# A row gradient in three slots: the second and third load of each group become one transfer

## The chip, the cores and the metric

The kernel runs on one core of one Trainium2 chip. The metric is the device time of one execution in microseconds (us). A core has engines that run instruction streams of their own; here VectorE (DVE) does the arithmetic, GpSimd (POOL) some very small operations, and SyncE (SP) issues all transfers between the chip's main memory (HBM) and its working memory (SBUF, 128 partitions). TensorE and ScalarE do nothing. A transfer is issued by one instruction on SP and is carried by 16 DMA engines; its semaphore says when all of it has landed.

## The reference

```python
x = np.random.randn(8192, 8192).astype(np.float32)
return np.gradient(x, axis=1)
```

Each row is differentiated along its 8192 columns: inside, `(x[j+1] - x[j-1]) / 2`; at the two ends, the plain differences `x[1] - x[0]` and `x[8191] - x[8190]`. The input and the output have 268.44 MB each.

## The kernel before

The 8192 rows are cut into 32 tiles (`nsets`) of 256 rows: 128 partitions with R = 2 rows each, so a tile has W = 16384 numbers, 64 KB, in each partition, 8.39 MB in all. Tiles come in groups of NB = 3. Within a group, partition p holds six rows that follow each other in HBM; tile k of the group is the k-th pair of them. `x_sets[i]` and `out_sets[i]` are the views of tile i in the input and the output. The last group has two tiles.

Three slots of SBUF (`slot0` to `slot2`) hold a tile each; tile i lies in slot i % 3, from element SH = 64 on. The result of a tile is written into the same slot, 64 elements further down, from element 0 on, and is stored from there. [...]

What happens with tile i, with the lines that do it:

- `load(i)` (line 55) issues its load on SP. From tile 3 on it needs the store of tile i - 3 to have landed, as that frees the slot.
- Line 65: POOL takes the four plain differences at the ends of the two rows into `ends`. It waits for the load.
- Line 71: DVE makes half the difference of the two neighbours, over the whole 16382 numbers at once. It waits for POOL's four differences, and so for the load.
- Line 82: the four end values are copied over the result's ends, on POOL for some tiles (i % 5 is 1 or 3, but not the last two tiles), on DVE for the others.
- Line 84: SP issues the store of the slot.

The order is written by hand (`tc.manual_schedule()`): each engine runs its instructions in the order of the program. SP's queue so reads: loads of tiles 0, 1, 2; stores 0, 1, 2; loads 3, 4, 5; stores 3, 4, 5, and so on. An instruction that waits holds back all that stand behind it in its engine's queue. `chain` names for each step the earlier step that it needs; the order of all else within a slot follows from that.

Of the kernel before, what the change touches and what calls it, by code (L numbers as in the profile page):

```python
# [1 line left out]

# [4 lines left out]


@with_exitstack
def kernel(  # L10
    ctx: ExitStack,
    tc: tile.TileContext,
    x: bass.AP,
    out: bass.AP,
):
    nc = tc.nc
    P = nc.NUM_PARTITIONS
    n, m = x.shape
    R = 2
    NB = 3  # L20
    SH = 64
    W = R * m
    nsets = n // (P * R)
    f32 = x.dtype

    def sets(a):
        found = []
        for first in range(0, nsets, NB):
            q = min(NB, nsets - first)
            rows = a[first * P * R : (first + q) * P * R, :].rearrange("(p q) m -> p (q m)", p=P)  # L30
            found += [rows[:, k * W : (k + 1) * W] for k in range(q)]
        return found

    x_sets, out_sets = sets(x), sets(out)

    pool = ctx.enter_context(tc.tile_pool(name="pool", bufs=1))
    pad = pool.tile([P, 32], f32, name="pad", tag="pad")
    slots = [pool.tile([P, SH + W], f32, name=f"slot{k}", tag=f"slot{k}") for k in range(NB)]
    ends = pool.tile([P, nsets, R, 2], f32, name="ends", tag="ends")
    loads, stores = [], [None] * nsets  # L40
    in_front = {}

    def chain(i, ins, *needed):
        group, engine = f"slot{i % NB}", ins.ins.engine
        keep = [o.ins for o in needed]
        if in_front.get(engine, (None,))[0] == group:
            keep.append(in_front[engine][1])
        tc.declare_no_dep(ins.ins, group=group, keep=keep, reason="implied by the needed step")
        tc.add_to_no_dep_group(group, ins.ins)
        in_front[engine] = group, ins.ins  # L50
        return ins

    def load(i):
        b = slots[i % NB]
        ins = nc.sync.dma_start(out=b[:, SH : SH + W], in_=x_sets[i])  # L55
        loads.append(chain(i, ins, *([stores[i - NB]] if i >= NB else [])))

    with tc.manual_schedule():
        for i in range(NB):
            load(i)  # L60
        for i in range(nsets):
            b = slots[i % NB]
            xin = b[:, SH : SH + W].rearrange("p (t m) -> p t m", m=m)

            ins = nc.gpsimd.tensor_sub(  # L65
                out=ends[:, i, :, :],
                in0=xin[:, :, 1 : m : m - 2],
                in1=xin[:, :, 0 : m - 1 : m - 2],
            )
            at = [chain(i, ins, loads[i])]  # L70
            ins = nc.vector._custom_dve(  # L71
                dve_ops.TENSOR_TENSOR_REDUCE_SUB_MAX,
                out=b[:, 1 : W - 1],
                in0=b[:, SH + 2 : SH + W],
                in1=b[:, SH : SH + W - 2],
                s0=0.0,
                s1=0.5,
            )
            halved = chain(i, ins, *at)
            res = b[:, 0:W].rearrange("p (t m) -> p t m", m=m)  # L80
            placer = nc.gpsimd if i % 5 in (1, 3) and i < nsets - 2 else nc.vector
            ins = placer.tensor_copy(out=res[:, :, 0 : m : m - 1], in_=ends[:, i, :, :])  # L82
            placed = chain(i, ins, halved)
            ins = nc.sync.dma_start(out=out_sets[i], in_=b[:, 0:W])
            stores[i] = chain(i, ins, placed)
            if i % NB == NB - 1:
                for k in range(i + 1, min(i + 1 + NB, nsets)):
                    load(k)


# [1 line left out]
_INS = ['x']  # L92
_OUTS = [((8192, 8192), 'float32')]


# [23 lines left out]
```

## Time and profile before

| | |
|---|---|
| time, median of 3 runs | 1246.33 us (1245.98 to 1246.47) |
| the profiled execution: time | 1246.23 us |
| the profiled execution: span, first to last instruction | 1244.3 us |
| DVE busy | 554.6 us, 45% of the span |
| POOL busy | 8.9 us, 1% |
| one pass of line 71 on DVE | 17.22 us, 32 times |
| transfers issued on SP | 32 loads and 32 stores |
| load, issue to landing, median | 57.9 us |
| store, issue to landing, median | 40.4 us |
| moved over the span | 431 GB/s in the mean |

Each line of the profile's groups names a line of the kernel, an engine and an operation with what it writes and reads. "Waits" give who waited for whom, with the total, the number of times and the longest. The timeline gives start and duration in us; what was idle before, and what ended that idle time, stands in square brackets; several issues that follow each other are merged into one line with their number. "SPq" is SP's instruction queue, "to landing" the time from an issue to the moment when all of its data is there. The trace also holds a record of each DMA packet with its start, duration and size, from which the movement of a single DMA engine can be followed.

### The profile page before, as it was taken

Reading aid. Unit: us, or ns where it says so; the run is one execution under the profiler, and the core shown is the slowest. Engines: PE = TensorE matmul, PEld = TensorE weight load, DVE = VectorE, ACT = ScalarE, POOL = GpSimd, SP = SyncE. Lnnn points to the kernel's source line nnn. Section 1 sums busy time; section 2 is a strip of 40 time slices with the busy share of each in tenths; the row PEclk is TensorE's granted clock in tenths of the full one; section 3 lists DMA queues with packets and bytes.
Section 4 is the critical chain, followed back from the end, with each engine's and each line's share of the span. In section 5 each row is a group of like instructions: output and inputs, shape, how many; then the busy total and the mean of one; then the engine's idle time right before and its main releaser. Section 6 shows DMA issues by size and latency. Waiting matters only on the chain.

```text
span 1244.3 us, 237 instructions
## 1 busy us (share of the span) xinstructions
DVE 554.6 (45%) x52; POOL 8.9 (1%) x48
## 2 busy tenths in 40 slices
DVE  2850583069009603850582079009603840591082
POOL 0000000000000000000000000000000000000000
DMA  9999999999999999999999999999999999999999
GB/s 404 438 436 423 421 438 438 438 438 436 434 423 430 434 438 438 430 436 432 428 434 436 432 436 434 438 436 430 432 428 438 436 434 438 434 434 430 430 409 404
DMA packets 9217, 536.88 MB, mean 431 GB/s; under 512 B 1024, under 2 KB 1024, under 8 KB 1024
## 3 DMA queue, kind: packets, MB, share of 16 engines
q1 hardware_dynamic: 9216, 536.88, 99.8%
q14 instruction: 1, 0.01, 0.0%
HBM read 268.44 MB, written 268.44 MB: 431 GB/s over the span
## 4 chain that ended last, share of the span: by engine, by line
another core or an unknown queue 74%; DVE 18%; DMA 3%; issue 2%; POOL 1%; SPq 0%; POOLq 0%
DVE slot L71 18%; DMA slot<-in_x_dram 3%; POOL ends L65 0%; POOL slot L82 0%; SPq L55 0%; POOLq L114 0%; DVE slot L82 0%
## 5 line engine op out<-in xcount | busy, mean ns | idle before, releaser
L71 DVE CUSTOM_DVE_ANT_0 slot<-slot 128x16382 f32<-128x16382 f32 x32 | 551.2, 17224 | 667.2 <-POOL ends L65 667.2
L65 POOL TENSOR_TENSOR ends<-slot 128x4 f32<-128x4 f32 x32 | 6.4, 200 | 988.1 <-DMA slot<-in_x_dram 988.1
L82 POOL COPY slot<-ends 128x4 f32<-128x4 f32 x12 | 2.3, 192 | 207.9 <-DVE slot L71 207.9
L82 DVE COPY slot<-ends 128x4 f32<-128x4 f32 x20 | 3.4, 172 | 0.7
L103 POOL MEMSET const-bfloat16-1.0<- 128x1 bf16 x1 | 0.1, 102 | 0.0
L103 POOL MEMSET const-uint8-127<- 128x1 uint8 x1 | 0.1, 102 | 0.0
L103 POOL MEMSET const-float32-0.0<- 128x1 f32 x1 | 0.1, 99 | 0.2 <-issue 0.2
L103 POOL MEMSET const-float32-1.0<- 128x1 f32 x1 | 0.1, 99 | 0.0
## 6 DMA issues: line engine op xcount, KB each, us to landing
slot<-in_x_dram SPq DMA_DIRECT2D x32, 57.9
out_dram<-slot SPq DMA_DIRECT2D x32, 40.4
```

The lines of the kernel that those rows point to most:

```text
L65: ins = nc.gpsimd.tensor_sub(out=ends[:, i, :, :], in0=xin[:, :, 1 : m : m - 2], in1=xin[:, :, 0 : m - 1 : m - 2],)
L71: ins = nc.vector._custom_dve(dve_ops.TENSOR_TENSOR_REDUCE_SUB_MAX, out=b[:, 1 : W - 1], in0=b[:, SH + 2 : SH + W], in1=b[:, SH : SH + W - 2],
L82: ins = placer.tensor_copy(out=res[:, :, 0 : m : m - 1], in_=ends[:, i, :, :])
L103: nc = _bacc.Bacc("TRN2", target_bir_lowering=False, num_devices=1)
```

## The change

The first slot becomes a tile of its own (`one`), and the second and third become one SBUF tile (`two`) that holds both, each with its 64 elements of room ahead as before. The first tile of a group is loaded as before. The second and third are loaded by one transfer of 2 x 64 KB a partition (`load_rest`): in HBM the two pieces follow each other directly, in SBUF they lie a slot apart. This transfer needs the stores of both tiles that were in the two slots before it. The last group, which has two tiles, loads them one by one as before. The stores, the arithmetic and the order of compute stay.

```diff
-    slots = [pool.tile([P, SH + W], f32, name=f"slot{k}", tag=f"slot{k}") for k in range(NB)]
+    one = pool.tile([P, SH + W], f32, name="one", tag="one")
+    two = pool.tile([P, NB - 1, SH + W], f32, name="two", tag="two")
+    slots = [one] + [two[:, k, :] for k in range(NB - 1)]
...
     def load(i):
-        b = slots[i % NB]
-        ins = nc.sync.dma_start(out=b[:, SH : SH + W], in_=x_sets[i])
+        ins = nc.sync.dma_start(out=slots[i % NB][:, SH : SH + W], in_=x_sets[i])
         loads.append(chain(i, ins, *([stores[i - NB]] if i >= NB else [])))
 
+    def load_rest(i):
+        rows = x[(i - 1) * P * R : (i + NB - 1) * P * R, :].rearrange("(p q) m -> p (q m)", p=P)
+        rest = rows[:, W : NB * W].rearrange("p (k w) -> p k w", w=W)
+        ins = nc.sync.dma_start(out=two[:, :, SH : SH + W], in_=rest)
+        for k in range(i, i + NB - 1):
+            chain(k, ins, *([stores[k - NB]] if k >= NB else []))
+            loads.append(ins)
+
+    def load_group(i):
+        load(i)
+        if i + NB <= nsets:
+            load_rest(i + 1)
+        else:
+            for k in range(i + 1, nsets):
+                load(k)
+
     with tc.manual_schedule():
-        for i in range(NB):
-            load(i)
+        load_group(0)
...
             if i % NB == NB - 1:
-                for k in range(i + 1, min(i + 1 + NB, nsets)):
-                    load(k)
+                load_group(i + 1)
```

## The prediction

> **What bounds the kernel now.** I read the page first (busy shares, slices, DMA queues), then the waits of the engines and of SP's queue, then the timeline of one group and of the last two tiles, and last the trace's DMA packet records, packet by packet.
>
> From the page:
>
> ```profile
> span 1244.3 us, 237 instructions
> DVE 554.6 (45%) x52; POOL 8.9 (1%) x48
> DMA  9999999999999999999999999999999999999999
> DMA packets 9217, 536.88 MB, mean 431 GB/s; under 512 B 1024, under 2 KB 1024, under 8 KB 1024
> q1 hardware_dynamic: 9216, 536.88, 99.8%
> ```
>
> DVE works less than half of the time; the one DMA queue has packets on its 16 engines for 99.8% of the span. The packet records give the grain: 8,192 packets of 65,536 B, eight per DMA engine and transfer, the median lasting 2.418 us and one starting 2.415 us after the other. So a transfer of one tile takes 8 x 2.415 = 19.32 us, load or store alike, and the 64 of them take 1,236.5 us of the 1,244.3. Only the rest, 7.8 us, can be won; anything that leaves the DMA engines without work costs directly.
>
> The waits, of the engines and then of SP's queue:
>
> ```profile
> POOL ends L65 <- DMA slot<-in_x_dram: 988.1, 32, 77.2
> DVE slot L71 <- POOL ends L65: 667.2, 32, 60.1
> ...
> SPq L84 <- DVE slot L82: 525.5, 20, 55.9
> SPq L55 <- DMA out_dram<-slot: 372.9, 29, 19.1
> SPq L84 <- POOL slot L82: 299.0, 12, 36.7
> ```
>
> Columns: total us, times, longest. POOL waits for loads and DVE for POOL; SP waits for compute before stores and for stores before loads. These waits cost nothing as long as another transfer is in flight. Whether one is can be read from one group in the timeline (tiles 3, 4, 5, which I call A, B, C: slots 0, 1, 2):
>
> ```profile
> 139.69 0.20 POOL L65 TENSOR_TENSOR ends<-slot 128x4 f32<-128x4 f32 x1 [77.15 <-DMA slot<-in_x_dram]
> 139.92 17.22 DVE L71 CUSTOM_DVE_ANT_0 slot<-slot 128x16382 f32<-128x16382 f32 x1 [59.92 <-POOL ends L65]
> 157.21 0.19 POOL L82 COPY slot<-ends 128x4 f32<-128x4 f32 x1 [17.32 <-DVE slot L71]
> 157.43 39.24 SPq L84 DMA_DIRECT2D out_dram<-slot  x3
> 159.01 0.20 POOL L65 TENSOR_TENSOR ends<-slot 128x4 f32<-128x4 f32 x1 [1.60 <-DMA slot<-in_x_dram]
> ...
> 178.64 0.20 POOL L65 TENSOR_TENSOR ends<-slot 128x4 f32<-128x4 f32 x1 [19.44 <-DMA slot<-in_x_dram]
> ...
> 197.94 39.04 SPq L55 DMA_DIRECT2D slot<-in_x_dram  x3
> ```
>
> A, B and C land at 139.62, 158.94 and 178.58, a transfer apart. A's store is issued at 157.43 and lands at 197.92: it stood behind loads B and C, so the queue serves in order. At each issue one transfer is in flight and another queued. The one place where that fails is the end:
>
> ```profile
> 1185.59 0.20 POOL L65 TENSOR_TENSOR ends<-slot 128x4 f32<-128x4 f32 x1 [77.06 <-DMA slot<-in_x_dram]
> 1185.82 17.23 DVE L71 CUSTOM_DVE_ANT_0 slot<-slot 128x16382 f32<-128x16382 f32 x1 [59.83 <-POOL ends L65]
> 1203.08 0.17 DVE L82 COPY slot<-ends 128x4 f32<-128x4 f32 x1
> 1203.28 19.61 SPq L84 DMA_DIRECT2D out_dram<-slot  x2
> ```
>
> Tile 30 lands at 1185.52 while only load 31 is queued, and its store is issued 17.76 us later. In the packet records the last load packets end between 1201.39 and 1204.51 on the 16 engines, and the store's packets start between 1204.13 and 1204.52: the early engines stand idle up to 2.9 us, and the latest, which sets the end, has no gap.
>
> **The change, part by part.** The sum is made against the profiled execution: 1246.23 us, its span 1244.3 and 1.9 around it; it is 0.1 us under the median, 1246.33.
>
> *Fewer issues.* Twenty loads become ten. SP spends 0.34 us on each, 3.4 us in all, while it waits 1,197 us in the rows above: nothing. Between transfers the packet records show no gap (load 0 ends at 21.75 on the first engine, load 1 starts at 21.75): joining two loads removes no idle time.
>
> [...]
>
> *The joined transfer.* Per engine it has 16 pieces of 64 KB in place of two times 8: the two slots stay apart in SBUF, so no piece grows. No row shows this form, two pieces in one partition running. Above, it can't beat the packet pace (0 us gained); below, I take 0 too, since loads and stores, with opposite ends, already have the same 2.415. B's data is usable only when the slowest engine has finished both, one transfer (19.32) later than now.
>
> *Its double wait.* SP issues it when both store B and store C have landed, not B's at store B's landing. Behind the wait in SP's queue stands store A of the next group, due some 37 us later (load A 19.3, then 17.8). Load A, issued as soon as store C is, is in flight meanwhile: store C lands about 0.3 us after its last packet, an issue takes 0.85 to 1.0 us to its first packet (1203.28 to 1204.13), and load A lasts 19.3: 18 us to spare. Load A itself no longer waits at all, as store A lands before store C is issued.
>
> *Store B, the tight place.* When the pair lands, only store A is queued. Call M the moment when the slowest engine ends the pair. Store A keeps it busy until M + 19.32. Store B's first packet comes at M + 0.33 (last packet to landing: 1185.19 to 1185.52) + 17.76 (landing to issue, as for tile 30; 17.81 where POOL places the ends, as at 139.62 to 157.43) + 0.85 to 1.0 = M + 18.94 to 19.14. The slowest engine has 0.18 to 0.38 us to spare, in all ten groups. Faster engines run dry and wait; that costs nothing, as at the end of before. Cost 0, by a thin margin.
>
> [...]
>
> *C's compute.* It starts when DVE is through with B, not 2 us after it. Where POOL places B's ends (tiles 1, 13, 16, 28) C's subtraction stands behind that copy on POOL, some 0.5 us more. Store C is due at M + 38.6 and issued near M + 36. Nothing.
>
> *Drift, the only moving term.* The 16 engines don't run in step. At each change from load C to store A the last load packet is lengthened on some of them: by 1.02 us on the mean at the first change, then by 0.19, 0.02, 0.12, 0.30, 0.12, 0.13, 0.03, 0.00, 0.04; nowhere else by over 0.05 but at the start. The latest end moves from 62.00 (load 2) to 1204.51 (load 31), 59 transfers of 19.32 = 1139.88 later: 2.63 us of lengthening in nine changes, 0.29 each. In the new kernel the dry wait at store B brings the engines together again in each group, to within some 0.4 us. Then each change may cost what it costs engines in step: at least 0, at most 1.00 (the first change, latest end 41.68 to 62.00 less 19.32). I take 0.34, the second change (158.60 to 178.26 less 19.32): its engines lay 0.63 us apart and it is no first. 9 x (0.34 - 0.29) = +0.45 us.
>
> The last two tiles and the start are as before. Sum: 1246.23 + 0.45 = 1246.7 us.
>
> **The rivals.**
>
> *In step (slower).* Each change costs 1.00 like the first: 9 x (1.00 - 0.29) = +6.4, 1252.6 us. For it: then the engines lay 0.6 us apart, and the lengthening shrinks as the drift grows. Against it: at the second change they lay as close and it was a fifth; the first is also the first write of the program. It passes 0.2% from 0.57 us per change on. Chance 0.14.
>
> *Store B too late (slower).* If the path from the pair's last packet to store B's first is x longer than summed, ten groups lose 10 (x - 0.28). It passes 0.2% from x = 0.53 on; at 0.7 it gives 1250.4, and with no cover at all 10 x 17.8 = 178 us, 1424. For it: the margin is a hundredth of a group. Against it: every link was measured in this trace. [...]
>
> *The lengthening goes (faster).* In before, SP issues store B (176.7) just while the last packets of load C run (174.9 to 177.9); engines that ended before that issue were lengthened by 0.1 at most at the later changes. In the new kernel nothing is issued during the pair's last packets. If that is the cause, 2.63 us go, and up to 3.6 with the first change: 1243.6 to 1242.6. Against it: at the ninth change (986.5 to 991.7) the issue fell in as well and nothing was lengthened. Chance 0.15 of passing 0.2%.
>
> [...] Chance under 0.01.
>
> **How the numbers follow.** 0.2% is 2.5 us, about what a measurement of this kernel can tell from no change: from 1243.8 to 1248.8 counts as none. The likeliest case, chance 0.58, lies in this band whole: 1244.2 to 1248.7, from lengthenings between 0.06 and 0.56. Slower by over 0.2%: 0.14 + 0.13 = 0.27. Faster: 0.15. The range runs from 1243.2 (most of the lengthening gone) to 1251.5 (0.87 us per change, or store B 0.8 late), and leaves out some 0.08 at each end.
>
> **What would show it.** In the new profile: 54 transfers, 9,057 packets (160 small ones fewer), DMA at 9 in all slices; a group still taking 116 us; DVE with the two passes of a pair back to back, then idle for some 42 us up to A and 21 us between A and the pair; the ends of the 16 engines within a microsecond of each other in all groups; packets of 2.418 us in the pair. Wrong are: slices under 430 GB/s once a group with a gap on all 16 engines before store B (store B too late), lengthened last packets of the pair near 1 us (in step), or a pair's packets of another duration than 2.418 us, of which no row here speaks.

## The result, and the profile after

The changed kernel takes 1261.49 us (median of 4 runs, 1261.22 to 1262.03), the kernel before 1246.2 us beside it: a ratio of 1.0123, 95% interval 1.0106 to 1.0141. It is 15.3 us slower. The forecast was 1246.7 us, its range ended at 1251.5.

The profiled execution took 1262.03 us, 15.8 more than that of before. From its page:

```profile
span 1260.1 us, 226 instructions
DVE 554.0 (44%) x52; POOL 8.3 (1%) x48
DMA  9999999999999999999999999999999999999999
GB/s 416 416 433 433 433 404 433 429 433 433 433 431 435 399 433 433 420 445 399 433 433 433 433 433 399 433 433 433 433 406 426 433 433 433 433 406 427 433 433 399
DMA packets 9057, 536.88 MB, mean 426 GB/s; under 512 B 864, under 2 KB 864, under 8 KB 864
...
q1 hardware_dynamic: 9056, 536.87, 99.8%
```

DVE works as long as before (554.0 us against 554.6), and the DMA queue still has packets under way for 99.8% of the span. The engines move less with them: the mean went from 431 to 426 GB/s, and among slices of 433 there stand some of 399 to 406. One group in the timeline (tiles 3, 4, 5, again A, B, C; the issues of stores B and C are one line):

```profile
140.53 0.20 POOL L81 TENSOR_TENSOR ends<-one 128x4 f32<-128x4 f32 x1 [60.25 <-DMA one<-in_x_dram]
...
158.27 0.35 SPq L100 DMA_DIRECT2D out_dram<-one  x1
180.19 0.35 POOL L81 TENSOR_TENSOR ends<-two 128x4 f32<-128x4 f32 x2 [21.95 <-DMA two<-in_x_dram]
180.42 17.22 DVE L87 CUSTOM_DVE_ANT_0 two<-two 128x16382 f32<-128x16382 f32 x1 [22.44 <-POOL ends L81]
197.68 0.17 DVE L98 COPY two<-ends 128x4 f32<-128x4 f32 x1
197.76 17.22 DVE L87 CUSTOM_DVE_ANT_0 two<-two 128x16382 f32<-128x16382 f32 x1
197.88 17.66 SPq L100 DMA_DIRECT2D out_dram<-two  x2
215.01 0.17 DVE L98 COPY two<-ends 128x4 f32<-128x4 f32 x1
215.59 1.23 SPq L56 DMA_DIRECT2D one<-in_x_dram  x1
238.93 0.39 SPq L62 DMA_DIRECT2D two<-in_x_dram  x1
258.28 0.20 POOL L81 TENSOR_TENSOR ends<-one 128x4 f32<-128x4 f32 x1 [77.74 <-DMA one<-in_x_dram]
```

The order of events is the one forecast: the pair lands at 180.12, store B is issued 17.76 us later at 197.88, the two passes of DVE stand back to back, the load of A follows store C at once and the next pair waits for store C's landing. But from A to A it is 117.75 us (140.53 to 258.28); before it was 116.24 (139.69 to 255.93). The stretches between A's arrivals, first of the changed kernel, then of before (columns: stretch, its length, busy time of DVE and POOL with the number of instructions, clock, DMA share, GB/s):

```profile
140.53:258.28 117.75, 51.91 (x5) 0.74 (x5) 1.00 1.00 427
258.28:376.06 117.78, 51.74 (x4) 0.92 (x5) 1.00 1.00 427
376.06:494.00 117.94, 51.91 (x5) 0.74 (x4) 1.00 1.00 427
```

```profile
139.69:255.93 116.24, 52.01 (x5) 0.79 (x4) 1.00 1.00 433
255.93:371.89 115.96, 51.84 (x4) 0.98 (x5) 1.00 1.00 434
371.89:488.16 116.27, 52.01 (x5) 0.80 (x5) 1.00 1.00 433
```

That is 1.5 to 1.8 us more per group, and there are ten groups. The packet records say where. (They don't name the engine; a packet that starts within some ns of another's end is taken as the next one of the same engine, which here gives 16 chains of equal length.) Lengthening is what a packet lasts beyond the usual 2.418 us, as a mean over the 16 engines, in the last packets of a transfer:

```
                                             before           after
load C or the pair, then store A, 1st change  1.02             1.18
  the nine later changes                      0.00 to 0.30     0.98 to 1.15
store C, then load A, ten changes             0.00             0.59 to 0.68
load A, first packet, after store C           0.02 at most     0.06 to 0.17
latest end of load 2 to that of load 31       1142.51          1158.10
  beyond 59 transfers of 19.32 us             2.63             18.22
```

18.22 - 2.63 = 15.6 us: nearly the whole difference of 15.8 between the two executions. In the mean over the 16 engines, 16.7 of the changed kernel's 18.4 us lie in lengthened packets at the changes of direction in the queue, from loads to stores and back, and 1.3 us in gaps between packets, most of them before store B. The packets in between last 2.418 us in the pair as elsewhere. No row of busy time shows the lengthening, since a lengthened packet counts as busy: the DMA share is 1.00 in all six stretches above.

### The profile page after: what moved, and what is told of

Read it like the earlier page. It is cut to its first block, busy times and chain, and to the rows that moved or that the text cites. A ratio compares the mean times of both kernels' runs of the same rounds, so it can differ in the third digit from the quotient of the medians.

```text
span 1260.1 us, 226 instructions
## 1 busy us (share of the span) xinstructions
DVE 554.0 (44%) x52; POOL 8.3 (1%) x48
## 2 busy tenths in 40 slices
DMA packets 9057, 536.88 MB, mean 426 GB/s; under 512 B 864, under 2 KB 864, under 8 KB 864
## 3 DMA queue, kind: packets, MB, share of 16 engines
q1 hardware_dynamic: 9056, 536.87, 99.8%
## 4 chain that ended last, share of the span: by engine, by line
DMA 35%; DVE 34%; another core or an unknown queue 26%; issue 2%; POOL 1%; SPq 0%; POOLq 0%
DMA one<-in_x_dram 35%; DVE two L87 29%; DVE one L87 5%; POOL ends L81 0%; SPq L100 0%; DVE two L98 0%; POOL two L98 0%; POOL one L98 0%; POOLq L129 0%
## 5 line engine op out<-in xcount | busy, mean ns | idle before, releaser
L87 DVE CUSTOM_DVE_ANT_0 two<-two 128x16382 f32<-128x16382 f32 x21 | 361.7, 17222 | 227.6 <-POOL ends L81 227.6
L87 DVE CUSTOM_DVE_ANT_0 one<-one 128x16382 f32<-128x16382 f32 x11 | 189.5, 17224 | 456.0 <-POOL ends L81 456.0
L81 POOL TENSOR_TENSOR ends<-two 128x4 f32<-128x4 f32 x21 | 3.9, 198 | 344.5 <-DMA two<-in_x_dram 344.5
```

The source lines that it names most:

```text
L81: ins = nc.gpsimd.tensor_sub(out=ends[:, i, :, :], in0=xin[:, :, 1 : m : m - 2], in1=xin[:, :, 0 : m - 1 : m - 2],)
L87: ins = nc.vector._custom_dve(dve_ops.TENSOR_TENSOR_REDUCE_SUB_MAX, out=b[:, 1 : W - 1], in0=b[:, SH + 2 : SH + W], in1=b[:, SH : SH + W - 2],
```

## The experiments

Most kernels of the study are read by one quantity. The **lead** of a transfer is how far ahead of need it reaches the queue: from 0.9 us after its issue (1203.28 to 1204.13 and later, at the end of before) to the moment when the first of the 16 engines ends the transfer in front (its landing there less 0.3 us, as the pair's last packet above ends at 179.81 and its landing is at 180.12). In before the stores of the ten full groups have leads of 16.6 to 20.1 us. In the changed kernel store B has -0.54 to -0.17 and store C 1.7 to 2.0 us. The table holds what the profiled executions show, the sections the edits.

```
kernel          lead of store   lead of store    lengthening        lengthening     median us
                B               C                store C to load    load to store
                                                                    (after the 1st)
before          16.8 to 20.1    16.6 to 19.1     0.00               0.11            1245.55
wait_only       17.0 to 20.0    16.9 to 19.1     0.00               0.07            1245.63
join_half        6.2 to  8.3     7.9 to 10.2     0.00               0.08            1245.68
join_split2      5.9 to  9.2     7.7 to 11.0     0.00               0.06            1246.72
before_split2   25.7 to 29.6    25.7 to 28.6     0.00               0.09            1246.39
join_trim3       1.4 to  2.6     3.1 to  4.6     0.00               0.10            1247.18
late_c          18.5 to 20.2    -0.5 to  1.9     0.37               0.69            1256.05
join_split       6.7 to  9.2    -0.1 to  1.6     0.34               0.83            1255.85
join_trim       -0.5 to  0.4     1.9 to  2.3     0.36               0.94            1256.97
join_trim15     -0.5 to  1.1     1.7 to  3.0     0.47               0.85            1258.92
late_c2         19.7 to 20.1    -0.5 to  0.2     0.61               0.93            1260.29
after           -0.5 to -0.2     1.7 to  2.0     0.64               1.03            1261.49
sep_late        -0.5 to -0.2     1.7 to  2.0     0.68               0.95            1262.3
```

(The time of before was taken anew beside each set of kernels: 1245.55 here, 1245.92, 1245.61 and 1245.56 in others; the ratios go by these. Where a store is in halves, the leads are those of both. Leads and lengthenings are those of one profiled execution, the time is the median of several. They lie close together but for join_trim3, whose profiled execution took 1245.17 us and was one of its fastest.)

### The joined transfer, or what it does to the order?

**sep_late.** Three loads as before; only the end differences of B wait for load C as well.

```diff
             at = [chain(i, ins, loads[i])]
+            if i % NB == 1 and i + 1 < nsets:
+                tc.add_manual_dep(
+                    ins.ins,
+                    loads[i + 1].ins.name,
...
```

> Three loads of their own as in before, but the end differences of each group's second tile, and so its pass and its store, wait for the third tile's load too, as they do in the changed kernel. Theory 1 (the dry queue at store B brings the 16 DMA engines in step, and in step they lose about 1.0 us at the change from loads to stores and 0.7 at the change back): as slow as the changed kernel, 1260 to 1263 us, last packets of load C lengthened by about 1.0 and those of store C by about 0.65 in each group. Theory 2 (the joined transfer itself, two pieces in one partition, makes the changes of direction dear): 1246 to 1247 us, lengthenings as in before.

Measured: 1262.3 us (1261.9 to 1262.87), ratio 1.0135 (1.012 to 1.015). All of the loss is there without a joined transfer. Its timeline has the changed kernel's order:

```profile
140.36 0.20 POOL L65 TENSOR_TENSOR ends<-slot 128x4 f32<-128x4 f32 x1 [60.29 <-DMA slot<-in_x_dram]
...
180.01 0.35 POOL L65 TENSOR_TENSOR ends<-slot 128x4 f32<-128x4 f32 x2 [21.94 <-DMA slot<-in_x_dram]
180.24 17.22 DVE L78 CUSTOM_DVE_ANT_0 slot<-slot 128x16382 f32<-128x16382 f32 x1 [22.43 <-POOL ends L65]
...
258.15 0.20 POOL L65 TENSOR_TENSOR ends<-slot 128x4 f32<-128x4 f32 x1 [77.79 <-DMA slot<-in_x_dram]
```

B's and C's end differences stand together at 180.01, and the next A comes at 258.15, 117.79 us after the last at 140.36. Theory 2 falls: the form of the transfer costs nothing.

**wait_only.** The other half of the change alone: load B waits for store C too.

```diff
+        if i >= NB and i % NB == 1 and i + 1 < nsets:
+            tc.add_manual_dep(
+                ins.ins,
+                stores[i + 1 - NB].ins.name,
...
```

> The kernel before, with one thing of the change: the load of each group's second tile also waits for the store of the third, as the joined transfer must. Compute and stores keep their times. In step: the queue doesn't run dry, so 1245 to 1247 us, no gaps, lengthenings as in before. A theory that the later issue of the loads leaves the queue too short would have it at 1255 us or more.

Measured: 1245.63 us, ratio 0.9999 (0.999 to 1.0008), lengthenings as in before. The double wait is hidden, as the prediction had it.

**join_half.** The changed kernel with half a pass over B.

```diff
+            upto = W // 2 if i % NB == 1 and i + 1 < nsets else W
             ins = nc.vector._custom_dve(
                 dve_ops.TENSOR_TENSOR_REDUCE_SUB_MAX,
-                out=b[:, 1 : W - 1],
-                in0=b[:, SH + 2 : SH + W],
-                in1=b[:, SH : SH + W - 2],
+                out=b[:, 1 : upto - 1],
+                in0=b[:, SH + 2 : SH + upto],
+                in1=b[:, SH : SH + upto - 2],
```

> The changed kernel, but DVE's pass over each joined pair's first tile covers only the first of its two rows a partition, so its store is issued 8.6 us earlier and the queue can't run dry there. The second row of these tiles is not computed. Theory 1 (in step by the dry queue): no gaps before store B, the engines drift, lengthenings shrink as in before, 1243 to 1249 us. Theory 2 (the joined transfer itself): 1260 to 1263 us, as the transfers are the same.

Measured: 1245.68 us, ratio 1.0001 (0.9992 to 1.001). With the same transfers, and stores B and C issued earlier, the whole loss is gone. So it hangs on when the stores reach the queue.

### Is it being in step?

**start_stagger.** Three small loads ahead of the first load of before, over 4, 8 and 12 engines.

```diff
+    def stagger():
+        first = 0
+        for k in (4, 8, 12):
+            nc.sync.dma_start(out=spare[first : first + k, :], in_=x[first : first + k, 0:3584])
+            first += k
...
+        stagger()
         for i in range(NB):
             load(i)
```

> The kernel before, with the same three small loads once, ahead of its first load: the engines start some 0.5, 1.1 and 1.6 us apart. Theory 1 (in step) also for the first change: its lengthening falls from 1.0 to under 0.3 us, and the later ones stay small; 1244 to 1247 us. Theory 3 (the first change is dear because it is the first write of the program): it stays near 1.0 us; 1246.5 to 1249 us.

Measured: 1248.1 us, ratio 1.002 (1.0011 to 1.003). The first change's lengthening went from 1.02 to 0.00, so theory 3 falls: the first write of the program can be free. The time did not get better. It lies 2.5 us above its control and in the range that theory 3 gave, but for another reason: the first packets of load 0 were lengthened by 1.9 us, and starts from 2.94 to 6.12 us set the engines back. That looked like being in step, and was not yet decided: the first packets had paid instead.

**start_small.** One spare load over 8 engines behind load 0.

```diff
         for i in range(NB):
             load(i)
+            if i == 0:
+                nc.sync.dma_start(out=spare[0:8, :], in_=x[0:8, 0:2688])
```

> The kernel before, with one spare load over 8 of the 16 DMA engines behind its first load, 10.5 KB for each of them: it sets these 8 some 0.4 us back, once. In step: the first change's lengthening of 1.0 us falls under 0.5, the 0.4 us come on top; 1244.5 to 1246 us, against some 1245.6 before. If 0.4 us doesn't part them enough: 1246 us or a little more.

Measured: 1245.79 us, ratio 0.9999 (0.999 to 1.0009): the time expected. The first change again costs nothing, but with the engines only 0.5 us apart, and 0.85 us stand in the first packets of load 1. So the distance is not what decides: 0.5 us apart cost 0.9 to 1.2 us in other kernels here.

**join_trim.** B's pass shorter by 0.5 us (`upto` is used as in join_half).

```diff
+            upto = W - 476 if i % NB == 1 and i + 1 < nsets else W
```

> The changed kernel, DVE's pass over each pair's first tile shorter by 476 of 16,382 elements, 0.50 us; these 476 differences are not computed. Store B so reaches the DMA engines some 0.8 us before the slowest of them needs it, not 0.3. If being in step is what costs and engines 0.6 to 0.8 us apart escape most of it (as at the second change of before, 0.19 us at 0.63 us apart): lengthenings under 0.4 us, few gaps, 1245 to 1250 us. If each dry wait costs, however short: 1258 us or more.

Measured: 1256.97 us, ratio 1.0089 (1.0074 to 1.0104): between the two expectations. After its second group no engine has a gap before store B any more, and still the changes cost 0.3 and 0.9 us. A gap isn't needed.

**join_split.** All the work, B in two halves (`halves` is 2 for the second tile of a group).

```diff
+            for h in range(halves):
+                lo = h * H
...
+                    out=b[:, lo + 1 : lo + H - 1],
...
+                ins = nc.sync.dma_start(out=out_sets[i][:, lo : lo + H], in_=b[:, lo : lo + H])
```

> The changed kernel with all of its work, but each pair's first tile is computed and stored in two halves, a row a partition each, so its first half is in the queue some 8.6 us earlier. In step: no gap before it, the drift comes back, 1244 to 1248 us with the joined transfer and its wait left as they are. If the joined transfer cost anything of its own: 1255 us or more.

Measured: 1255.85 us (1252.04 to 1258.16), ratio 1.0078 (1.0058 to 1.0097). B's halves have leads of 6.7 us or more, no engine has a gap before them, the engines drift 2 us apart, and still the changes cost up to 0.6 and 1.2 us. Here the theory of engines in step fell. The time is the one expected if the joined transfer had a cost of its own, but sep_late has the whole loss without one. What was left is store C: its lead shrinks from 1.55 to about 0 as the early engines draw ahead, and the cost grows with that. In the first four groups no engine has a gap before store C either; later one to five engines do in some groups, of up to 0.45 us.

```
group                     1     2     3     4     5     6     7     8     9     10
lead of store C           1.55  1.24  0.55  0.39  0.14  0.07  0.16  -0.10 0.10  -0.02
lengthening at store C    0.00  0.15  0.18  0.23  0.46  0.48  0.33  0.61  0.40  0.52
at the pair that follows  0.15  0.44  0.93  0.81  1.21  1.04  0.97  0.85  1.08
```

### The lead

Theory 4, formed here: a transfer has to be in the queue some 2 us, about the length of a packet (2.418 us), before the first engine needs it; if not, the next changes of direction are dear, with or without a gap.

**late_c.** The kernel before with its own loads; two copies of C onto itself ahead of its pass make store C late, and nothing else.

```diff
+            if i % NB == 2:
+                for w in (W, W):
+                    ins = nc.vector.tensor_copy(out=b[:, SH : SH + w], in_=b[:, SH : SH + w])
+                    at = [chain(i, ins, *at)]
```

> The kernel before, with two copies of each group's third tile onto itself on DVE ahead of its pass, at an estimated 8.6 us each: store C comes to the queue some 2 us before store B ends there, not 19 us. Nothing else of the order changes, and the 16 engines have drifted apart as in before. Theory 4 (no gap is needed: a transfer that is queued less than about 2 us ahead, the length of a packet, makes the next two changes of direction dear): 1246 to 1252 us, at the edge. In step by a dry queue (theory 1): no gap, so 1245 to 1247 us.

Measured: 1256.05 us (1250.32 to 1261.91), ratio 1.0084 (1.0061 to 1.0108). A group from its timeline; the three stores are one line, whose end, 565.14, is that of store C's issue:

```profile
507.28 57.86 SPq L88 DMA_DIRECT2D out_dram<-slot  x3
...
529.89 17.42 DVE L73 COPY slot<-slot 128x16384 f32<-128x16384 f32 x2 [3.57 <-POOL ends L65]
547.35 17.22 DVE L75 CUSTOM_DVE_ANT_0 slot<-slot 128x16382 f32<-128x16382 f32 x1
...
607.06 0.20 POOL L65 TENSOR_TENSOR ends<-slot 128x4 f32<-128x4 f32 x1 [77.20 <-DMA slot<-in_x_dram]
```

The two copies cost 17.42 us of DVE, 8.7 each, in time in which it lay idle anyway (busy for 45% of the span in before), and store C comes 0.25 us ahead of need in this group. Over the groups its lead falls as in join_split, from 1.85, 1.32 and 0.67 to between 0.25 and -0.54, and the lengthenings rise from 0.00, 0.02 and 0.11 to 0.39 and more at the change back, and up to 1.01 at the next. So one late store is enough, with engines 2 us and more apart. The time lies above theory 4's range too: that range took the lead to stay near 2 us, and drift ate it.

**late_c2.** A third copy, `(W, W, 2800)`.

> The same with a third, short copy, an estimated 1.5 us: store C is queued some 0.4 us ahead. Theory 4: the last packets of store C and of load C are lengthened by 0.3 to 0.7 and 0.8 to 1.1 us, 1253 to 1261 us, without a gap. Theory 1: 1245 to 1248 us.

Measured: 1260.29 us, ratio 1.0119 (1.0104 to 1.0134); the third copies took 1.6 us each (190.1 us for all 30 copies, less 20 of 8.69), and the lengthenings are 0.61 and 0.93, as expected of theory 4.

**join_trim15, join_trim3.** The changed kernel again, B's pass shorter by 1,428 and by 2,856 elements.

> The changed kernel, DVE's pass over each pair's first tile shorter by 1,428 elements, 1.5 us; these differences are not computed. Store B is queued some 1.3 us ahead, store C 3 us. Theory 4: between the kernels, 1247 to 1255 us. Theory 1: 1245 to 1247 us, as no engine waits.

Measured: 1258.92 us, ratio 1.0109 (1.0094 to 1.0124). More than in join_trim, a miss: the leads of 0.8 to 1.1 in three groups go with 0.01 to 0.27 at store C, but the engines drift apart, the first one needs store B earlier, the lead falls to -0.2 and less, and the full price returns. A margin that drift eats is none.

> The same, shorter by 2,856 elements, 3.0 us: store B is queued some 2.8 us ahead, store C 4.5 us, both by more than a packet. Both theories: 1245 to 1248 us; if it is still 1252 or more, more than a packet's lead is needed.

Measured: 1247.18 us, ratio 1.0027 (1.0008 to 1.0046), single executions from 1245.11 to 1254.81: the edge. The profiled one (1245.17 us), with leads of 1.4 and more, has no lengthening at store C at all. Two of the ten took 1253.9 and 1254.81, over the 1252 us named beforehand; their packets were not recorded, so what leads they had is open.

**join_split2 and before_split2.** All the work, the joined transfer, B and C in halves (`halves` is 2 for second and third tiles); and the same halves in before.

> The changed kernel with all of its work; both tiles of each pair are computed and stored in halves, a row a partition each, so that all stores are queued 8 us or more ahead. Theory 4 (a lead shorter than a packet is the whole cost): as fast as before, 1244 to 1248 us, lengthenings as in before. If part of the cost is the joined transfer's or the late landing's own: 1250 us or more.

> The kernel before with the same halves: second and third tile of each full group in halves, loads as before. All leads are longer than a packet already: 1244 to 1247 us, the same as before, by every theory; another time would say what the halves themselves do.

Measured: 1246.72 us, ratio 1.001 (1.0001 to 1.002), and 1246.39, ratio 1.0007 (0.9998 to 1.0016). From the joined one's timeline:

```profile
139.66 0.20 POOL L81 TENSOR_TENSOR ends<-one 128x4 f32<-128x4 f32 x1 [77.08 <-DMA one<-in_x_dram]
...
178.34 0.35 POOL L81 TENSOR_TENSOR ends<-two 128x4 f32<-128x4 f32 x2 [20.97 <-DMA two<-in_x_dram]
...
187.49 26.71 SPq L106 DMA_DIRECT2D out_dram<-two  x4
...
255.63 0.20 POOL L81 TENSOR_TENSOR ends<-one 128x4 f32<-128x4 f32 x1 [76.94 <-DMA one<-in_x_dram]
```

The first half of B is issued 9.2 us after the landing, not 17.8, each of the four halves has a lead of 5.9 us or more, and the group takes 115.97 us (139.66 to 255.63). The cost is that of the short lead: with a longer one the joined transfer is as fast as its control. The halves alone don't explain it, as join_half has no lengthening with whole stores. Neither beats the kernel before.

### One that told nothing

**join_stagger.** The small loads of start_stagger behind each store B of the changed kernel.

> The changed kernel, with three small loads into a spare tile behind each group's store B, over 4, 8 and 12 DMA engines, 14 KB for each engine: they set the engines some 0.5, 1.1 and 1.6 us apart after each dry wait, and cost the last ones these 1.6 us in each group (16 us in all). Theory 1 (in step): the last packets of the pair and of store C are lengthened by under 0.4 on the mean, what the stagger costs is won back, 1257 to 1264 us. Theory 2 (the joined transfer itself): lengthenings stay at 1.0 and 0.65 and the stagger comes on top, 1274 to 1279 us.

Measured: 1304.62 us, ratio 1.0476. The edit brought in what it was to measure: the small loads stand between stores, two changes of direction more per group, with last packets of some 3 us, and their 14 KB pieces took 1.3 us in the median, not 0.5. The time is far above both ranges. Nothing follows from it on either theory.

## Why the prediction was wrong, point by point

- *What bounds the kernel*: right. It is the DMA engines, with packets under way for 99.8% of the span; the double wait (wait_only), the joined form (sep_late, join_split2), the fewer issues and C's later pass are free, as costed. No run shows a gain from fewer transfers: join_half, with ten fewer, took 1245.68 us against 1245.55.
- *Store B, the tight place*: the working was right, its price was not. Store B is issued at landing + 17.76, the early engines stand idle by up to 0.7 us, 0.1 in the mean over the 16, and the latest has no gap: its 0.3 to 0.4 us to spare are about those of the sum. The step that failed is "Cost 0, by a thin margin": it took a transfer to be early enough when its first packet is there at the end of the one in front. The runs show that it had to be there some 1.5 us before the first engine's end for the change back to cost nothing, and that a miss is paid later, at the next change back to loads (0.64 us) and the change after that (1.03).
- *Drift, the only moving term*: the step saw that the changes from loads to stores are where time goes, took 0.34 us for them and had 1.0 as its other bound; they cost 1.03. That changes from stores to loads could cost anything was missed: before shows 0.00 in all ten of them, with all its leads at 16.6 us or more, and no row of it could have priced them. They are 0.64 + 0.10 us a group.
- *Rival "in step"*: it named the place and the size of the first term (9 x (1.00 - 0.29) = 6.4 us of the 15.6), by a cause that fell. Lengthenings shrink in before not because the engines drift apart; late_c has them 2 us apart and pays 0.37 and 0.69 us.
- *Rival "the lengthening goes"*: its condition came, its effect didn't. In the group shown SP issues nothing between store A (158.27) and store B (197.88), so nothing during the pair's last packets, and they are lengthened by 1.00 us.
- *Rival "store B too late"* (the 0.13 among the chances): it looked at the right margin with the wrong price, x beyond the margin, times ten. The price isn't proportional: store B was within the margin and cost the whole.
- *What to see*: 54 transfers, 9,057 packets, back-to-back passes, 2.418 us in the pair came as said; the group of 116 us didn't, and "lengthened last packets of the pair near 1 us" was named as the mark of a wrong forecast.

## What to carry to other kernels

Here, where the DMA queue is the bound, it was not enough that a transfer is there when its predecessor ends: join_trim, after its second group without a gap before store B, took 11 us more than its control (1256.97 against 1245.92). So look for each transfer at how long before its predecessor's end it is issued, and keep that several us above the time from issue to first packet (about 0.9 us here), as drift between the engines eats some of it (store B's lead in before falls from 20.1 to 16.8 us over ten groups). With leads of 5.9 us and more the change from stores to loads cost 0.00 in all kernels here; join_trim3, whose profiled execution has 1.4 to 4.6, took from 1245.11 to 1254.81 us. The change that makes two tiles land together took lead from the stores behind them (16.6 us and more before, -0.5 to 2.0 after), though the page still has the DMA at 9 in all 40 slices. The loss hid in busy time (99.8% for the queue in both kernels): compare the time from one group to the next and the durations of single packets, not shares.

## What the runs showed of the hardware

Shown, in these kernels: a store that joins the queue too shortly before the first DMA engine needs it (with a lead of 1.35 us or less in the table) lengthens the last packets before the next changes of direction, with or without a gap. The profiled executions of all these kernels together, by the shortest lead among the group's stores B and C (us, mean over the 16 engines; groups 1 to 9 of each kernel, with the change back that follows the group's stores and the change after that):

```
shortest lead     stores to loads   loads to stores
under 0           0.53 to 0.71      0.81 to 1.15
0 to 0.6          0.18 to 0.56      0.59 to 1.21
0.6 to 1.35       0.01 to 0.27      0.09 to 0.91
1.5 to 2.7        0.00              0.01 to 0.34
5.9 and more      0.00              0.00 to 0.35
```

Between 0.6 and 1.35 us it is uncertain what a group pays. The row from 1.5 us on rests nearly alone on one execution of join_trim3, and slower ones of that kernel show that such leads are no safe margin. The 0.87 to 1.18 us at the first change of every kernel that starts with its plain loads fit a price for a short lead, as the first transfer has no lead at all, and so do 0.85 us in load 1's first packets (start_small), but that was not tried by itself.

The eleventh change from loads to stores, in the last group, is in no table. There the store is not yet queued when the last packets of load 31 start (in the changed kernel they start at 1217.18 to 1217.76, the store is issued at 1218.95). These packets are lengthened by 0.04 us at most in all kernels of the table above, and by 0.00 in the changed kernel, though the group ahead of it had a short lead. So a price at a change was seen only where the next transfer was already in the queue.

Open: why the price falls due at the changes of direction and not at once. No run here shows it.
